# Hybrid diffusion backbone: the state chain's products as one block matrix or as two 64x64 tiles

## The chip, the cores and the metric

The kernel runs on one core of one Trainium2 chip. The metric is the device time of one execution in microseconds, lower is better. A time is the median of several runs; beside it stands one execution that was taken with the hardware profiler, from which all rows below come.

## The reference

One layer of a diffusion backbone over 256 context and 1024 latent tokens, width 1024, in float32. Three token mixers work beside each other on slices of the width (a recurrent mixer with 4 heads of 64, neighbourhood attention with 8 heads, a gated short convolution), one projection joins them, and a product-key expert layer follows. The part that matters here is the recurrent mixer. It keeps, for each head and each of two directions, a 64x64 state `S` that runs over the tokens:

```python
def step(S, inp):
    r_t, kk_t, v_t, w_t, b_t, k_t = inp
    sa = jnp.einsum('bhij,bhj->bhi', S, kk_t)
    S = S * w_t[:, :, None, :] - sa[..., None] * b_t[:, :, None, :] + v_t[..., None] * k_t[:, :, None, :]
    return S, jnp.einsum('bhij,bhj->bhi', S, r_t)
```

The state starts at zero, runs over the context and then over the latent tokens, forward in one direction and backward in the other. The outputs of the latent tokens from both directions are added and normalised.

## The kernel before, in words

The kernel turns the token-by-token recurrence into chunks of 64 tokens. `batch(step, d)` (from line 459 on) treats four chunks of one direction `d`: step 0 is the context, steps 1 to 4 are the latent tokens, so there are ten batches. The two heads of a pair share the 128 partitions: head 0 on partitions 0 to 63, head 1 on 64 to 127, and the index `h` runs over the two pairs. Matrices of a chunk are therefore 128x128 with two 64x64 blocks on the diagonal and zeros elsewhere. They are made by masks (`bn`, `gk`, L555), by transposes of block tiles (`kt`, and the first half of `bn`, L572 and L573), or by additions into the diagonal blocks of a tile that was cleared once (`pr`, L638 to L645).

A batch first builds its operands (lines 467 to 578), solves a triangular system (L580 to L630: `lp`, `lt`, `lx`, `x12`) and makes the transfer matrix `pr`. Only then comes the state chain, lines 649 to 669, which is what the change touches. For each of the four chunks and each pair `h` it makes the new state `M` from three products that gather in one region of PSUM (`mc`, from `kt`, `bn` and `pr`; L658, L659, L661), which ScalarE scales into SBUF (L663). For latent batches it also makes the chunk's output from three products (`yc`, from `gk`, `bn` and `pr`; L667 to L669). The third product of each trio reads the state that the chunk before left. The operand held in the array is the 128x128 block matrix; the moved operand has 64 columns. All of them are float32. Work of other kinds stands beside the batches in the program: the input projections (`pj`, L158 to L160), the neighbourhood attention (`pw`, `pc`, `pt`, `po`, L806 to L839) and, after the last batch, the rest of the projections, the output projection and the expert layer with its gathers.

The order of instructions on each engine is not written by hand. The tile framework plans it by simulating the program, so products of several batches, of the projections and of the attention stand mixed on TensorE's queue, which TensorE works off in order (its weight loads run ahead of its products). Waits between engines are semaphores that the framework places; in a trio only the last product signals ScalarE.

Of the kernel before, what the change touches and what calls it, by code (L numbers as in the profile page):

```python
# [19 lines left out]
P = 128  # L20
# [34 lines left out]
def hybrid_kernel(ctx: ExitStack, tc: tile.TileContext, A: dict, out: bass.AP, dbg=None):  # L55
    nc = tc.nc
# [118 lines left out]
    def bank(name, tag):  # L175
        return pw1.tile([P, 512], F32, tag=tag, name=name, bufs=NBANK[tag])
# [67 lines left out]
    for m in range(8, 16, 2):  # L244
        w = sm_.tile([P, 2, KD, P], F32, tag="aw", name=f"aw{m}", bufs=4)
        nc.sync.dma_start(w, A["ada_w"][:, m - 8:m - 6])
        ps = bank(f"ada{m}", "ra")
        for j in range(2):
            for k in range(KD):
                nc.tensor.matmul(ps[:, 2 * j:2 * j + 2], w[:, j, k, :], scc[:, k, :],  # L250
                                 start=k == 0, stop=k == KD - 1)
# [187 lines left out]
    def rot(name, shape, n, init=lambda t: nc.vector.memset(t, 0.0)):  # L439

        if name not in RN:
            ts = [cw.tile(shape, F32, name=f"{name}{i}") for i in range(n)]
            for t in ts:
                init(t)
            RN[name] = [ts, 0]
        r = RN[name]
        r[1] += 1
        return r[0][(r[1] - 1) % n]
# [7 lines left out]
    def b2(ap):  # L456
        return ap.unsqueeze(2).to_broadcast([P, 4, 2, 64])

    def batch(step, d):
        g = 0 if step == 0 else (step if d == 0 else 5 - step)  # L460
        c0, t0, lat = 4 * g, 256 * g, g > 0
# [12 lines left out]
        for h in range(2):  # L474
            ci = 2 * d + h

            def gt(name, shape, bufs=1, h=h):
                return gp.tile(shape, F32, tag=name, name=f"{name}_{step}{d}{h}", bufs=bufs)
# [12 lines left out]
            if last:  # L491
                rb = rot("kx", [P, 4, P], 1)
                bps = bank(f"bo{g}{h}", "ra")
                for a in range(2):
                    q_ = slice(64 * a, 64 * a + 64)
# [56 lines left out]
            bn, gk = gt("bn", [P, 4, 256], 4), gt("gk", [P, 4, P], 4)  # L552
# [14 lines left out]
            kt = gt("kt", [P, 4, P], 4)  # L567
            rx = gt("rx", [P, 4, 192], 3)
            for src, dst in ((kx, rx[:, :, 0:P]), (bb, bn[:, :, 0:P]), (kb, kt)):
                ps = bank(f"tr_{step}{ci}", "ra")  # L570
# [3 lines left out]
            ps = bank(f"lkv_{step}{ci}", "ra")  # L574
# [13 lines left out]
        for h in range(2):  # L588
            s, ci = S[h], 2 * d + h
# [5 lines left out]
            ps = bank(f"x0_{step}{ci}", "rb")  # L595
# [6 lines left out]
        for l in range(2):  # L602
            for h in range(2):
                s, ci = S[h], 2 * d + h
                ps = bank(f"lp_{step}{ci}{l}", "rb")
                for u in range(4):
                    nc.tensor.matmul(ps[:, u * P:(u + 1) * P], s["E"][:, u, :], s["X"][:, u, :], start=True, stop=True)
                pm = s["gt"]("pm", [P, 4, P])
                nc.vector.tensor_mul(pm, ps.rearrange("p (c b) -> p c b", c=4),
                                     cst[:, C_L16 + l, :].unsqueeze(1).to_broadcast([P, 4, P]))  # L610
                ps = bank(f"lt_{step}{ci}{l}", "rb")
# [8 lines left out]
        for h in range(2):  # L620
            s, ci = S[h], 2 * d + h
            x12 = s["gt"]("x12", [P, 4, 192], 2)
            for u2 in range(2):
                ps = bank(f"x12_{step}{ci}{u2}", "rb")
                for j in range(2):
                    u = 2 * u2 + j
# [3 lines left out]
        for h in range(2):  # L630
            s, ci = S[h], 2 * d + h
            pr = rot("pr", [P, 4, 256], 2)
            na_ = 2 if lat else 1
            for u2 in range(2):
                ps = bank(f"pr_{step}{ci}{u2}", "rb")
                for j in range(2):
                    u = 2 * u2 + j
                    nc.tensor.matmul(ps[:, j * 256:j * 256 + na_ * P], s["x12"][:, u, 0:P], s["bn"][:, u, :na_ * P], start=True, stop=True)  # L638
                us = slice(2 * u2, 2 * u2 + 2)
                for a in range(2):  # L640
                    q_ = slice(64 * a, 64 * a + 64)
# [8 lines left out]
        for i in range(4):  # L650
            for h in range(2):
                s, ci = S[h], 2 * d + h
                u = i if d == 0 else 3 - i
                v_, x2_ = s["vS"][:, u, :], s["x12"][:, u, P:]
                M = Mst.get(ci)
                if step < 4 or i < 3:
                    pm = mch[:, h * 256 + u * 64:h * 256 + u * 64 + 64]
                    nc.tensor.matmul(pm, s["kt"][:, u, :], v_, start=True, stop=False)  # L658
                    nc.tensor.matmul(pm, s["bn"][:, u, 0:P], x2_, start=False, stop=M is None)  # L659
                    if M is not None:  # L660
                        nc.tensor.matmul(pm, s["pr"][:, u, 0:P], M, start=False, stop=True)  # L661
                    Mn = gp.tile([P, 64], F32, tag=f"M{ci}", name=f"M_{step}{ci}{i}", bufs=2)
                    nc.scalar.activation(Mn, pm, AF.Copy, scale=s["tot"][:, u:u + 1])  # L663
                    Mst[ci] = Mn
                if lat:
                    py = ych[:, h * 256 + u * 64:h * 256 + u * 64 + 64]
                    nc.tensor.matmul(py, s["gk"][:, u, :], v_, start=True, stop=False)  # L667
                    nc.tensor.matmul(py, s["bn"][:, u, P:], x2_, start=False, stop=False)
                    nc.tensor.matmul(py, s["pr"][:, u, P:], M, start=False, stop=True)  # L669
        if not lat:  # L670
            return
        if last:
# [29 lines left out]
        for h in range(2):  # L702
            yd = rot("yd", [P, 4, P], 1)
            for a in range(2):
                q_ = slice(64 * a, 64 * a + 64)
                nc.vector.tensor_add(yd[q_, :, q_], vb[h][q_], y[q_, h])
            ps = bank(f"yo{h}{g}", "ch")
# [3 lines left out]
        nc.sync.dma_start(d_y[:, 0:2, tl:tl + 256], gs)  # L711

    batch(0, 0)
    batch(0, 1)
    rwkv_inputs(TBLK[1])
    batch(1, 0)
    load_h(*TBLK[2], 0)
    rwkv_inputs(TBLK[2])
# [369 lines left out]
    for q in range(2):  # L1088
        ps = bank(f"g2{q}", "pj")
# [191 lines left out]
    for e in range(P):  # L1281
# [16 lines left out]
        for t0, n in DBLK:  # L1298
            ps = bank(f"ds{e}_{t0}", "pj" if opened or t0 else "rb")[:, :n]
# [40 lines left out]
    for g in range(NGRP):  # L1340
# [20 lines left out]
        if g == NGRP - 1:  # L1361
            fins, fgen, ends = (), None, list(ENDS)
            for x, i in enumerate(LAST):
                if i < len(stay):
                    acc_of(i, stay[i], False, True)
                else:
                    ps = bank(f"dq{g}{i}", "ch")
# [13 lines left out]
        for r in range(nr):  # L1381
            ps = bank(f"dq{g}{r}", "ch")
# [100 lines left out]
```

## Time and profile before

| what | value |
|---|---|
| median of 3 runs | 3696.5 us (3678.78 to 3700.78) |
| profiled execution | 3709.2 us, span 3707.4 us |
| TensorE busy (products) | 3357.4 us, 91% |
| VectorE busy | 2921.6 us, 79% |
| ScalarE busy | 1564.8 us, 42% |
| GpSimd busy | 1391.3 us, 38% |
| mean granted TensorE clock | 0.95 |

In the rows, PE is TensorE's products and PEld its weight loads, DVE is VectorE, ACT ScalarE, POOL GpSimd. A row names the line, the operation, what it writes and what it reads (buffer numbers left out). A count such as x8 is the number of instructions. The duration of a product contains its way through the array, so products overlap each other in the rows; their pace is read from the starts of successive rows. The granted clock is a share of full speed: 1.00 is 2.4 GHz, 0.50 is 1.2 GHz.

### The profile page before, as it was taken

Reading aid. Unit: us, or ns where it says so; the run is one execution under the profiler, and the core shown is the slowest. Engines: PE = TensorE matmul, PEld = TensorE weight load, DVE = VectorE, ACT = ScalarE, POOL = GpSimd, SP = SyncE. Lnnn points to the kernel's source line nnn. Section 1 sums busy time; section 2 is a strip of 40 time slices with the busy share of each in tenths; the row PEclk is TensorE's granted clock in tenths of the full one; section 3 lists DMA queues with packets and bytes.
Section 4 is the critical chain, followed back from the end, with each engine's and each line's share of the span. In section 5 each row is a group of like instructions: output and inputs, shape, how many; then the busy total and the mean of one; then the engine's idle time right before and its main releaser. Section 6 shows DMA issues by size and latency. Waiting matters only on the chain.

```text
span 3707.4 us, 55747 instructions
## 1 busy us (share of the span) xinstructions
PE 3357.4 (91%) x19927; PEld 3031.5 (82%) x19927; DVE 2921.6 (79%) x6275; ACT 1564.8 (42%) x3039; POOL 1391.3 (38%) x1100
## 2 busy tenths in 40 slices
PE   7698898897879878989899999999998999999997
PEld 6587787886868757989899999999986778888885
DVE  7566657785685648989879999999876888888888
ACT  3453333442434433246244676676632333233332
POOL 3343232110053223445433335455542544443343
PEclk9899998998989889989999999999998999999998
DMA  6435543221565645798887879999998999999996
GB/s 249 129 114 163 161 138 96 65 64 55 171 198 170 205 163 174 272 312 304 299 281 260 284 287 347 344 367 369 341 353 300 345 339 340 345 346 349 339 345 230
DMA packets 405784, 928.08 MB, mean 250 GB/s; under 512 B 45569, under 2 KB 182145, under 8 KB 399873
## 3 DMA queue, kind: packets, MB, share of 16 engines
q1 hardware_dynamic: 248064, 408.81, 34.1%
q0 software_dynamic: 111920, 407.95, 30.6%
q10 hardware_dynamic: 45520, 107.76, 7.5%
q8 instruction: 157, 2.57, 0.3%
q14 instruction: 123, 1.00, 0.1%
HBM read 802.74 MB, written 121.63 MB: 249 GB/s over the span
## 4 chain that ended last, share of the span: by engine, by line
PE 31%; DVE 14%; DMA 8%; issue 7%; POOL 1%; ACT 1%; SPq 1%; DVEq 0%; ACTq 0%; POOLq 0%
PE ds L160 4%; PE ds L158 4%; PE ds L159 4%; DVE ru L1152 4%; PE dp L158 4%; PE dp L159 4%; PE dp L160 4%; PE gm L1067 2%; PE dq L159 2%; PE dq L160 2%; PE dq L158 2%; DMA rv<-in_peer_v_dram,idx 1%; DMA dws<-d_ge 1%; DMA ru<-in_peer_u_dram,idx 1%; DVE acc L1163 1%
## 5 line engine op out<-in xcount | busy, mean ns | idle before, releaser
L1135 POOL DMA_INDIRECT ru<-in_peer_u_dram,idx x384 | 513.8, 1338 | 735.2 <-ACT dqs L1387 172.7
L1135 POOL DMA_INDIRECT rv<-in_peer_v_dram,idx x384 | 498.8, 1299 | 700.5 <-ACT dqs L1387 237.0
L1152 DVE CUSTOM_DVE_ANT_0 ru<-ru,h 128x1024 f32<-128x1024 f32 x384 | 471.7, 1242 | 87.3 <-DMA ru<-in_peer_u_dram,idx 84.5
L1163 DVE SCALAR_TENSOR_TENSOR acc<-rv,gw,acc 128x1024 f32<-128x1024 f32 x381 | 488.7, 1283 | 38.0 <-DMA rv<-in_peer_v_dram,idx 34.4
L159 PE MATMUL dp<-dvls,dwhs 128*128 128x512 f32 x896 | 349.7, 391 | 1.1 <-DVE dvls L1269 1.1
L160 PE MATMUL dp<-dvhs,dwls 128*128 128x512 f32 x896 | 347.2, 390 | 0.0
L158 PE MATMUL dp<-dvhs,dwhs 128*128 128x512 f32 x896 | 318.7, 395 | 0.0
L208 POOL TENSOR_TENSOR wl<-w,wh 128x1024 fp32r<-128x1024 f32 x68 | 166.4, 2451 | 300.8 <-ACT wh L206 291.2
L158 PE MATMUL pj<-hbh,wh 128*128 128x512 f32 (+1 forms) x544 | 216.5, 399 | 19.5 <-ACT wh L206 13.8
L1302 ACT ACTIVATE ge<-ds 128x256 f32<-128x256 f32 (+1 forms) x256 | 111.1, 434 | 268.6 <-PE ds L160 221.8
L160 PE MATMUL pj<-hbh,wl 128*128 128x512 f32 (+1 forms) x544 | 213.8, 394 | 2.0 <-POOL wl L208 1.9
L159 PE MATMUL pj<-hbl,wh 128*128 128x512 f32 (+1 forms) x544 | 212.5, 391 | 2.1 <-POOL hbl L189 2.1
L158 PEld LDWEIGHTS dp<-dvhs,dwhs 128*128 128x128 f32 x896 | 171.1, 191 | 35.6
L159 PEld LDWEIGHTS dp<-dvls,dwhs 128*128 128x128 f32 x896 | 169.5, 189 | 36.9 <-DVE dvls L1269 1.5
L1272 ACT CAST dwhs<-dws 128x640 fp32r<-128x640 f32 x128 | 91.4, 731 | 254.0 <-DVE dws L1271 124.2
L160 PEld LDWEIGHTS dp<-dvhs,dwls 128*128 128x128 f32 x896 | 169.1, 189 | 35.3
L158 PE MATMUL dq<-dvhs,dwhs 128*128 128x512 f32 x384 | 151.3, 394 | 25.6 <-ACT dvhs L1268 23.6
L1269 DVE TENSOR_TENSOR dvls<-dvs,dvhs 128x1024 fp32r<-128x1024 f32 x128 | 155.3, 1220 | 24.5 <-ACT dvhs L1268 24.2
L1268 ACT CAST dvhs<-dvs 128x1024 fp32r<-128x1024 f32 x128 | 133.0, 1052 | 83.2 <-DMA dvs<-in_peer_v_dram 79.1
L1067 PE MATMUL gm<-oa,ob 128*128 128x128 f32 x1280 | 156.9, 275 | 1.6 <-DVE oa L1054 1.1
L1387 ACT COPY dqs<-dq 128x512 f32<-128x512 f32 x90 | 52.8, 587 | 249.7 <-PE dq L160 242.9
L1067 PEld LDWEIGHTS gm<-oa,ob 128*128 128x128 f32 x1280 | 152.5, 192 | 2.5 <-issue 1.4
(1990 smaller groups left out, 10266.1 us busy)
## 6 DMA issues: line engine op xcount, KB each, us to landing
du<-in_peer_ut_dram SPq DMA_DIRECT2D x128, 512.0 KB
dvs<-in_peer_v_dram SPq DMA_DIRECT2D x128, 512.0 KB
d_ge<-ge ACTq DMA_DIRECT2D x128, 320.0 KB
d_g<-gt ACTq DMA_DIRECT2D x40, 1024.0 KB
dgs<-d_g SPq DMA_DIRECT2D x32, 1280.0 KB
dws<-d_ge SPq DMA_DIRECT2D x128, 320.0 KB
w<-in_w_in_dram SPq DMA_DIRECT2D x68, 512.0 KB
wq<-in_q_w_dram SPq DMA_DIRECT2D x48, 512.0 KB
```

Source lines behind the costliest of these rows:

```text
L158: nc.tensor.matmul(ps, lh_, rh_, start=start, stop=False)
L159: nc.tensor.matmul(ps, lh_, rl_, start=False, stop=False)
L160: nc.tensor.matmul(ps, ll_, rh_, start=False, stop=stop)
L208: WE[0].tensor_tensor(wl, w, wh.bitcast(F32), op=OP.subtract)
L1067: nc.tensor.matmul(ps[:, t * P:(t + 1) * P], ob[:, q + t], oa[:, q + t], start=True, stop=True)
L1135: paced(nc.gpsimd.indirect_dma_start(out=r, out_offset=None, in_=A[tab], in_offset=bass.IndirectOffsetOnAxis(ap=idx[:, tt, s:s + 1], axis=0)))
L1152: yield from rows("peer_u", tt, lambda s, u: nc.vector.tensor_tensor_reduce(u, u, h2, 1.0, 0.0, OP.mult, OP.add, act[:, s:s + 1]))
L1163: nc.vector.scalar_tensor_tensor(acc, v, w[:, s:s + 1], acc, op0=OP.mult, op1=OP.add)
L1268: nc.scalar.copy(vh, v)
L1269: sv = nc.vector.tensor_tensor(vl, v, vh.bitcast(F32), op=OP.subtract)
L1272: nc.scalar.copy(wh, wt)
L1302: ev = nc.scalar.activation(ge[:, t0:t0 + n], ps, AF.Gelu_apprx_tanh)
```

## The change

Each product of the chain is issued twice, once for each head: the 64x64 block of the held operand against the 64 partitions of the moved operand, into the 64 partitions of the result. The order of the three terms stays, and within a term head 0 comes before head 1. Nothing else changes.

```diff
+    def heads2(ps, terms):
+
+        for i, (lt, rt) in enumerate(terms):
+            for a in range(2):
+                q_ = slice(64 * a, 64 * a + 64)
+                nc.tensor.matmul(ps[q_], lt[q_, q_], rt[q_], start=i == 0, stop=i == len(terms) - 1)
...
                 if step < 4 or i < 3:
                     pm = mch[:, h * 256 + u * 64:h * 256 + u * 64 + 64]
-                    nc.tensor.matmul(pm, s["kt"][:, u, :], v_, start=True, stop=False)
-                    nc.tensor.matmul(pm, s["bn"][:, u, 0:P], x2_, start=False, stop=M is None)
-                    if M is not None:
-                        nc.tensor.matmul(pm, s["pr"][:, u, 0:P], M, start=False, stop=True)
+                    heads2(pm, ((s["kt"][:, u, :], v_), (s["bn"][:, u, 0:P], x2_)) + (() if M is None else ((s["pr"][:, u, 0:P], M),)))
                     Mn = gp.tile([P, 64], F32, tag=f"M{ci}", name=f"M_{step}{ci}{i}", bufs=2)
                     nc.scalar.activation(Mn, pm, AF.Copy, scale=s["tot"][:, u:u + 1])
                     Mst[ci] = Mn
                 if lat:
                     py = ych[:, h * 256 + u * 64:h * 256 + u * 64 + 64]
-                    nc.tensor.matmul(py, s["gk"][:, u, :], v_, start=True, stop=False)
-                    nc.tensor.matmul(py, s["bn"][:, u, P:], x2_, start=False, stop=False)
-                    nc.tensor.matmul(py, s["pr"][:, u, P:], M, start=False, stop=True)
+                    heads2(py, ((s["gk"][:, u, :], v_), (s["bn"][:, u, P:], x2_), (s["pr"][:, u, P:], M)))
```

## Rows read from the trace of the kernel before

**Rows 1.** The page's first part: busy us, share of the span, instructions.
```profile
PE 3357.4 (91%) x19927; PEld 3031.5 (82%) x19927; DVE 2921.6 (79%) x6275; ACT 1564.8 (42%) x3039; POOL 1391.3 (38%) x1100
```
**Rows 2.** Busy time by stretch: us, each engine (instructions), PEclk, DMA share, GB/s.
```profile
250.00:905.00 655.00, 575.01 (x3847) 524.74 (x3845) 430.60 (x1208) 242.16 (x551) 151.76 (x175) 0.94 0.35 104
905.00:1385.00 480.00, 388.19 (x2252) 339.08 (x2253) 306.81 (x887) 199.79 (x388) 135.75 (x89) 0.87 0.58 179
756.00:760.00 4.00, 4.00 (x21) 4.00 (x21) 2.41 (x9) 0.81 (x2) 2.69 (x5) 0.51 0.49 146
```
**Rows 3.** TensorE's longest wait, 250 to 905 us: total, times, longest.
```profile
PE lt L613 <- DVE pm L609: 19.9, 7, 7.1
```
**Rows 4.** The chain's instructions by line: duration ns min/median/max, first and last start.
```profile
L658 PE MATMUL mc<-vS,kt x152: 217/273/421, 256.7 to 898.6; 128*128 128x64 f32 x152
L659 PE MATMUL mc<-x,bn x152: 275/275/421, 256.9 to 898.8; 128*128 128x64 f32 x152
L661 PE MATMUL mc<-M,pr x144: 275/275/421, 265.5 to 899.1; 128*128 128x64 f32 x144
L663 ACT ACTIVATE M<-mc,tots x76: 301/315/344, 258.1 to 899.4; 128x64 f32<-128x64 f32 x76
...
L667 PE MATMUL yc<-vS,gk x128: 219/275/421, 289.8 to 899.5; 128*128 128x64 f32 x128
L668 PE MATMUL yc<-x,bn x128: 219/275/287, 424.3 to 899.7; 128*128 128x64 f32 x128
L669 PE MATMUL yc<-M,pr x128: 219/275/422, 436.5 to 900.0; 128*128 128x64 f32 x128
```
**Rows 5.** Timeline of the last chain, one period: start us, us, engine, line, operation.
```profile
891.80 0.39 PE L658 MATMUL mc<-vS,kt 128*128 128x64 f32 x2
...
892.25 0.39 PE L661 MATMUL mc<-M,pr 128*128 128x64 f32 x2
...
892.67 0.31 ACT L663 ACTIVATE M<-mc,tots 128x64 f32<-128x64 f32 x1 [4.92 <-PE mc L661]
...
893.14 0.39 PE L658 MATMUL mc<-vS,kt 128*128 128x64 f32 x2
```
**Rows 6.** Timeline of TensorE's products, at 710 us and at 757 us.
```profile
710.12 1.00 PE L498 MATMUL bo<-cst,kx 128*128 128x2 f32 x8
710.98 0.85 PE L826 MATMUL pt<-cst,s 128*128 128x128 f32 x6
711.67 1.06 PE L613 MATMUL lt<-XT,pm 128*128 128x128 f32 x8
712.57 0.82 PE L627 MATMUL x<-rx,XT 128*128 128x192 f32 x4
...
756.80 1.92 PE L613 MATMUL lt<-XT,pm 128*128 128x128 f32 x8
758.51 1.72 PE L617 MATMUL lx<-pm,XT 128*128 128x128 f32 x8
```
**Rows 7.** Timeline of TensorE's products, where the chain meets other work, 744 us.
```profile
744.21 0.36 PE L806 MATMUL pw<-kh,qs 128*128 128x256 f32 x1
744.41 0.33 PE L658 MATMUL mc<-vS,kt 128*128 128x64 f32 x2
744.58 0.39 PE L659 MATMUL mc<-x,bn 128*128 128x64 f32 x2
...
745.02 0.39 PE L669 MATMUL yc<-M,pr 128*128 128x64 f32 x2
745.22 0.36 PE L807 MATMUL pw<-kl,qs 128*128 128x256 f32 x1
...
746.12 0.44 PE L658 MATMUL mc<-vS,kt 128*128 128x64 f32 x2
746.39 0.39 PE L659 MATMUL mc<-x,bn 128*128 128x64 f32 x2
```
**Rows 8.** Timeline of TensorE's weight loads, the start after a wait.
```profile
746.12 0.30 PEld L658 LDWEIGHTS mc<-vS,kt 128*128 128x128 f32 x2 [0.27 <-ACT M L663]
```

## The prediction

> **What bounds the kernel now.** I read the page's first part, then the busy time by stretch, then the waits of TensorE, then the rows of the edited lines. TensorE is the busiest engine over the whole span, with 91% [rows 1]. The products that the change touches all lie in the stage of the recurrent mixer, 250 to 905 us. There TensorE is busy for 575.0 of 655 us, 88%, and no other engine passes 66% [rows 2]. So its queue, which it works off in order, sets the stage: other batches, projections and attention stand between the products of the chain and fill the time in which those wait. The 80 us that are left are mostly waits inside the solve of a batch; the largest is 19.9 us, for the masked product on VectorE [rows 3]. The chain's own products hardly show there. ScalarE's step that makes the next state waits for TensorE, not the other way round. What TensorE gains or loses in these products therefore goes into the stage's end at nearly full size. I take 0.88 of it, the busy share, since the other 12% is slack in which a shorter or longer piece may vanish. The profile can't show that the delay reaches the end of the kernel, but the output of this stage is an input of everything after it, and TensorE is 81% busy in the next stretch too [rows 2], so I pass it on whole.
>
> **What the products cost.** Each call in float32 appears as two pairs of a weight load and a matmul, since lines 658 to 669 show 152, 152, 144 and three times 128 pairs, and only 76 new states [rows 4]. That is 832 pairs from 416 calls. In the last chain, where nothing else is on the chip, one chunk's six products for both head pairs (12 pairs) take 893.14 - 891.80 = 1.34 us [rows 5], 0.112 us a pair. All of them: 832 x 0.112 = 93 us of TensorE.
>
> What sets 0.112? Pairs that move 2 columns take (710.98 - 710.12) / 8 = 0.108 us, pairs that move 128 take (712.57 - 711.67) / 8 = 0.112, and pairs of 64, above, the same [rows 6]. So it isn't the moved columns. At the lower clock (0.51 in 756 to 760 us [rows 2]) the pair takes (758.51 - 756.80) / 8 = 0.214 us [rows 6], almost twice as much, so it isn't a cost of issuing either, which would not follow that clock. What these pairs share is the load of a 128-column operand.
>
> **The change, part by part.** It removes 416 calls and adds 832, each with half the rows, half the columns loaded, and the same 64 columns moved: 1,664 pairs in place of 832. ScalarE's step, the semaphore that releases it, the planes of PSUM and all DMAs stay. The result of a product is the same, since the block matrices hold zeros outside the two heads' blocks. No wait is added: the last pair of a group is still the one that releases ScalarE.
>
> *Price of a pair.* No row shows a load of fewer than 128 columns, so I bound it. Upper end: the load doesn't get shorter, and 1,664 x 0.112 = 186 us, +93. Lower end: a load of 64 columns takes half, 0.056 us, and the loads of the two tiles go side by side: 832 x 0.056 = 47 us, -47. Between them: half as long, and one after the other, as all loads here come: 1,664 x 0.056 = 93 us, no change. I take this one, since it is nearest to what rows show (work in proportion to the clock, one load behind the other). A fixed part beside it follows from the two clocks: twice 0.112 less 0.214 is 0.010 us by the pairs of 128 columns, and about nothing by those of 2. For the 832 extra pairs that is 0 to 8 us; I take +4.
>
> *Going in and out of the tiles.* The 832 pairs stand in 90 unbroken runs on TensorE's queue, between the first of 256.7 us and the last, of 80 pairs, at 891.2 us; 37 of them are of 12 pairs. So there would be some 180 changes between the whole array and its tiles. Lower end: nothing. A run begins 0.20 us after a product of another form and width, and the next begins 0.20 us after its last two pairs, without a gap (744.21 to 744.41, 745.02 to 745.22) [rows 7]. Upper end: TensorE must empty itself first. A product's latency is 275 ns at the median [rows 4], 0.163 us beyond its share of 0.112. And a load that couldn't be taken ahead shows its price once: after a wait for the state the first two pairs took 746.39 - 746.12 = 0.27 us [rows 7, 8], against 744.58 - 744.41 = 0.17 us otherwise: 0.10 us. Together 0.26 us a change, 47 us in all. I take one such uncovered load per run, 90 x 0.10 = 9 us, between the ends but nearer to the rows without a gap.
>
> The Trainium skill, in TensorEngine Tiling (Array Packing), Key Properties, says that a change of the tiling mode, as against a change of tile, drains TensorE. No run here shows it; by it the upper end of this term would hold, and it is the second rival below. The same section says that tiles are independent and can run weight loads and matmuls in parallel; by that the lower end of the pair's price would hold, the first rival below. The trace has no second tile to agree or disagree with.
>
> *Cover.* The latency of the chain itself costs nothing so far: ScalarE's step takes 0.31 us in a period of 1.34 [rows 5], beside products that don't need the new state. That cover stays, since the products of the state against the rest come last in the group as before. Were it gone, each step would wait 0.31 us for ScalarE and some more, 76 steps, at most 24 us, of which most lie beside other work.
>
> *Order.* The order of the queues comes from a planner that simulates the program. With other instructions it may place batches and projections differently. The whole idle time of the stage is 80 us [rows 2]; I give a reordering 15 us either way.
>
> **The sum.** (4 + 9) x 0.88 = +11 us. The profiled execution took 3709.2 us around a span of 3707.4, so it would take 3720. It stands 12.7 us above the median of the runs, 3696.5; on the median the forecast is 3707.5. A measurement of this kernel tells about 1%, 37 us, from no change, so this is no change.
>
> **The rivals.**
> 1. *The tiles load side by side.* The queue would hold 47 us less; with 9 for the changes, (9 - 47) x 0.88 = -33, 3663. For it: the two tiles share neither rows nor columns of the array. Against it: no row shows two loads at a time. With the dear changes of rival 2 as well, it ends near zero, which I count with the forecast.
> 2. *Every change of mode empties the array* (the other side). Place: the 90 runs between products of the whole array. Price: 47 us of uncovered latency and load, plus 4, times 0.88 = +45, 3741. For it: the runs are short, mostly 12 pairs or fewer. Against it: today's changes of form and width leave no gap [rows 7]. It decides from about 0.2 us a change; below that the result stays within 1%.
> 3. *A load costs the same for 64 columns.* +93 and 9, times 0.88 = +90, 3786. For it: pairs of all widths cost the same [rows 6]. Against it: that row varies only the moved columns.
> 4. The clock falls. It is 0.94 on the mean in this stage [rows 2], so it falls now and then already. No row says what products on tiles do to it; half of the chain's 93 us at the lower clock would add 47 us. It goes into the upper part of the range with rival 2.
>
> **How the numbers follow.** Forecast (loads in turn, changes cheap, or both effects dear and cancelling): 0.48, within about 15 us of 3707. Rival 1: 0.22, of which half falls below the 1% mark of 3660. Rivals 2 and 4: 0.20, most of it above 3733. Rival 3: 0.10. Range 3655 to 3745: it takes in the forecast, most of rival 1 and half of what lies above rival 2's price, and leaves out rival 3 and the tails. The chances: faster 0.12, the half of rival 1 with a little of reordering; slower 0.26, rival 3, most of rivals 2 and 4; the rest, 0.62, is within 1%.
>
> **What would show it.** Right: in the last, undisturbed chain a chunk for both head pairs still takes about 1.34 us with 24 pairs of 64 columns, 0.056 us apart, and the stage's end moves by less than 20 us. Rival 1: that period falls towards 0.7 to 0.9 us, until ScalarE's step shows as TensorE's wait. Rival 2: idle time of TensorE just before the first pair of each run and before the first whole-array load after it. Rival 3: a period of about 2.7 us. Rival 4: a granted clock well under 0.94 in the stage. The sum is wrong if TensorE's products shorten and the stage's end doesn't move, for then the waits in the solve were the bound.

## The result and the profile after

The changed kernel takes 3669.3 us (median of 5 runs, 3663.1 to 3677.9) where the kernel before, in 5 runs beside it, takes 3696.5: a ratio of 0.9937, 95% interval 0.9913 to 0.9960, so 23 us or 0.6% less. That is within the 1% that the prediction called no change and inside its range, but on the other side of zero from its sum of +11 us.

The page's first part of the kernel after:

```profile
span 3667.5 us, 57401 instructions
PE 3334.0 (91%) x20759; PEld 2986.6 (81%) x20759; DVE 2905.2 (79%) x6275; ACT 1561.9 (43%) x3038; POOL 1398.4 (38%) x1100
```

TensorE has 832 more products and loads than in [rows 1], and less busy time. The span is 39.9 us shorter than that of before, but the profiled execution of before stood 12.7 us above its median and this one is its median, so 27 us is what the two have to explain.

The chain's instructions, listed by tile (duration ns min/median/max, first and last start):

```profile
L464 PEld LDWEIGHTS mc<-vS,kt x304: 129/132/228, 252.0 to 878.7; 64*64 64x64 f32 x152
L464 PE MATMUL mc<-vS,kt x304: 218/218/366, 252.0 to 878.7; 64*64 64x64 f32 x152
...
L667 ACT ACTIVATE M<-mc,tots x76: 296/315/350, 253.4 to 879.3; 128x64 f32<-128x64 f32 x76
...
L464 PE MATMUL yc<-M,pr x256: 218/218/311, 425.1 to 879.8; 64*64 64x64 f32 x128
```

Against [rows 4] there are twice as many products, as the change says; each is 218 ns long instead of 275. The chain ends at 879.8 us, 20.2 us earlier than the 900.0 of before. (It also began 4.7 us earlier, ahead of anything that was edited.) Behind the chain 18.7 us were left at the last projection (1211.3 against 1230.0) and 27.1 at the first expert product (1483.4 against 1510.5).

How fast the pairs go stands in the timeline of the last chain, one period (start us, us, engine, line, operation, and in brackets the idle time and what ended it):

```profile
876.60 0.19 PEld L464 LDWEIGHTS mc<-vS,kt 64*64 64x64 f32 x4 [0.20 <-ACT M L667]
876.60 0.33 PE L464 MATMUL mc<-vS,kt 64*64 64x64 f32 x4
...
876.77 0.28 PE L464 MATMUL mc<-x,bn 64*64 64x64 f32 x4
...
876.88 0.28 PE L464 MATMUL mc<-M,pr 64*64 64x64 f32 x4
...
877.00 0.28 PE L464 MATMUL yc<-M,pr 64*64 64x64 f32 x4
...
877.12 0.28 PE L464 MATMUL yc<-vS,gk 64*64 64x64 f32 x4
...
877.21 0.32 ACT L667 ACTIVATE M<-mc,tots 128x64 f32<-128x64 f32 x1 [0.67 <-PE mc L464]
877.23 0.28 PE L464 MATMUL yc<-x,bn 64*64 64x64 f32 x4
...
877.58 0.33 PE L464 MATMUL mc<-vS,kt 64*64 64x64 f32 x4
```

Four pairs (two heads, two passes) start every 0.11 to 0.12 us: 877.23 - 876.77 = 0.46 us for sixteen, 0.029 us a pair. A product for both heads costs half of what it did. The period fell from the 1.34 us of [rows 5] to 877.58 - 876.60 = 0.98, of which the 24 pairs take about 0.70; then TensorE stands and waits for the new state. ScalarE's step, which was hidden, now shows as 0.20 us of idle time in each period of this undisturbed chain. In the busy stage it hardly does: the waits of TensorE for `M` are 1.6 us there, against 1.1 before.

What going in and out of the tiles costs stands in a busier place, in the same view, TensorE's products:

```profile
523.71 0.38 PE L614 MATMUL lp<-X,E 128*128 128x128 f32 x2
524.02 0.33 PE L464 MATMUL mc<-vS,kt 64*64 64x64 f32 x4
524.18 0.28 PE L464 MATMUL mc<-x,bn 64*64 64x64 f32 x4
524.30 0.28 PE L464 MATMUL mc<-M,pr 64*64 64x64 f32 x4
...
524.65 0.28 PE L464 MATMUL yc<-x,bn 64*64 64x64 f32 x4
524.86 0.71 PE L614 MATMUL lp<-X,E 128*128 128x128 f32 x4
```

and its weight loads:

```profile
523.59 0.31 PEld L614 LDWEIGHTS lp<-X,E 128*128 128x128 f32 x2
524.02 0.19 PEld L464 LDWEIGHTS mc<-vS,kt 64*64 64x64 f32 x4
524.13 0.20 PEld L464 LDWEIGHTS mc<-x,bn 64*64 64x64 f32 x4
...
524.86 0.63 PEld L614 LDWEIGHTS lp<-X,E 128*128 128x128 f32 x5
```

Within a run the loads are ahead of the products (524.13 against 524.18). At both ends they aren't: the first tile load and the first tile product begin together, and so do the first whole load and product behind the run. The second `lp` product starts at 523.81; without a change of mode the first tile product could follow 0.11 us later. From there to 524.86 are 0.94 us for 24 pairs that need 0.70. So one run costs 0.24 us for going in and out together. The 1,664 pairs stand in 97 unbroken runs. Counted in the same way, the 76 of them that have no wait and the full granted clock cost 0.24 us at the median; and at all 97 the first product, on the way in as on the way out, starts within 0.03 us of its load.

Both prices give the queue: 1,664 x 0.029 + 97 x 0.24 = 48 + 23 = 71.5 us where 93 stood, 21.5 less, and at the prediction's 0.88 a gain of 19 us. The busy time by stretch from the first chain product to the last, in the kernel before and in the kernel after:

```profile
256.70:900.00 643.30, 568.07 (x3807) 518.84 (x3805) 422.21 (x1185) 238.56 (x546) 151.76 (x175) 0.94 0.35 105
252.00:879.80 627.80, 562.44 (x4639) 491.26 (x4638) 418.61 (x1185) 238.11 (x546) 152.64 (x175) 0.93 0.36 108
```

The stage is 15.5 us shorter at a clock lower by 0.01. Length times granted clock is my estimate of the stage at full speed, good to some 3 us because the clock is given to two places; it falls from 605 to 584, by 21. That the chain's end came 20.2 us earlier, nearly the 19, is in part luck, since 4.7 of it lie ahead of the chain.

By stretch, as in [rows 2]:

```profile
250.00:905.00 655.00, 574.78 (x4682) 500.34 (x4680) 433.02 (x1226) 241.89 (x553) 152.64 (x175) 0.91 0.36 108
```

The same 655 us now hold the stage and 25 us of what follows, and the granted clock is 0.91 over them.

### The profile page after: what moved, and what is told of

Read it like the earlier page. It is cut to its first block, busy times and chain, and to the rows that moved or that the text cites. A ratio compares the mean times of both kernels' runs of the same rounds, so it can differ in the third digit from the quotient of the medians.

```text
span 3667.5 us, 57401 instructions
## 1 busy us (share of the span) xinstructions
PE 3334.0 (91%) x20759; PEld 2986.6 (81%) x20759; DVE 2905.2 (79%) x6275; ACT 1561.9 (43%) x3038; POOL 1398.4 (38%) x1100
## 4 chain that ended last, share of the span: by engine, by line
PE 37%; DVE 14%; DMA 5%; issue 4%; ACT 1%; POOL 1%; SPq 1%; ACTq 0%; DVEq 0%; POOLq 0%
PE dp L158 5%; PE dp L159 5%; PE dp L160 5%; PE ds L160 4%; PE ds L158 4%; PE ds L159 4%; DVE ru L1154 4%; PE gm L1069 2%; PE dq L158 2%; PE dq L159 2%; PE dq L160 2%; DVE acc L1165 1%; DMA rv<-in_peer_v_dram,idx 1%; DVE oa L1056 1%; DMA dws<-d_ge 1%
## 5 line engine op out<-in xcount | busy, mean ns | idle before, releaser
L1137 POOL DMA_INDIRECT ru<-in_peer_u_dram,idx x384 | 504.4, 1314 | 728.1 <-ACT dqs L1389 166.8
L1137 POOL DMA_INDIRECT rv<-in_peer_v_dram,idx x384 | 510.6, 1330 | 682.2 <-ACT dqs L1389 247.0
L1154 DVE CUSTOM_DVE_ANT_0 ru<-ru,h 128x1024 f32<-128x1024 f32 x384 | 475.7, 1254 | 82.1 <-DMA ru<-in_peer_u_dram,idx 81.9
```

Source lines behind the costliest of these rows:

```text
L1137: paced(nc.gpsimd.indirect_dma_start(out=r, out_offset=None, in_=A[tab], in_offset=bass.IndirectOffsetOnAxis(ap=idx[:, tt, s:s + 1], axis=0)))
L1154: yield from rows("peer_u", tt, lambda s, u: nc.vector.tensor_tensor_reduce(u, u, h2, 1.0, 0.0, OP.mult, OP.add, act[:, s:s + 1]))
```

## The experiments

The theory: the two tiles work side by side, 0.029 us a pair, because they share neither rows nor columns of the array; a run of them costs 0.24 us to enter and leave; and what the queue gains or loses reaches the end nearly whole. Its rivals: that the gain comes from another order of the planner rather than from the tiles, that the changes of mode cost nothing, or that the queue isn't the bound. In the expectations A is the theory and B the rival that the run is to tell from it, as each text says. Edits are against the kernel after, unless another is named. A time is set against the kernel before on the same chip, with the ratio and its 95% interval.

**Head by head, not term by term.**

```diff
-        for i, (lt, rt) in enumerate(terms):
-            for a in range(2):
+        for a in range(2):
+            for i, (lt, rt) in enumerate(terms):
```

> The same tile products, but all terms of head 0 of a trio first, then all of head 1, so that neighbours on the queue mostly share a tile. Theory A (only neighbouring products of different tiles run side by side): a trio of 12 pairs takes about 12 x 0.056 = 0.67 us, as the whole-array form does, with a little overlap where the tiles change; the gain of the changed kernel is lost and the in-and-out cost of the runs stays, so 10 to 20 us slower than before. Rival B (the engine looks far enough ahead to run both tiles' queues side by side whatever the order): a trio still takes about 0.35 us and the time stays with the changed kernel's, 0.6% below before.

3681.6 us, 0.9964 (0.9948 to 0.9980). The timeline of TensorE's products, last chain:

```profile
875.55 0.33 PE L464 MATMUL mc<-vS,kt 64*64 64x64 f32 x2
...
876.12 0.28 PE L464 MATMUL yc<-vS,gk 64*64 64x64 f32 x2
876.24 0.22 PE L464 MATMUL yc<-x,bn 64*64 64x64 f32 x1
876.25 0.27 PE L464 MATMUL yc<-vS,gk 64*64 64x64 f32 x1
876.30 0.22 PE L464 MATMUL yc<-x,bn 64*64 64x64 f32 x1
...
876.69 0.32 PE L464 MATMUL mc<-vS,kt 64*64 64x64 f32 x2
```

A period of 1.14 us; the 24 pairs themselves take 0.915 us, 0.038 each. Three products of one tile in a row let the other tile wait, yet not all the way to the 0.056 us of loads in turn: it lies between the two expectations. The two heads next to each other, as in the change, are worth something. The rows also settle a rival that the theory leaves open, that a 64x64 load takes a quarter of a 128x128 one (it holds a quarter as many numbers) and the loads still go in turn: while one tile has the queue to itself, its pairs start 0.06 us apart (two from 876.12 to 876.24), and when the other tile's first pair comes, it starts 0.01 us behind (876.25). So a pair of one tile takes about 0.058 us, half of a whole one, and 0.029 is two tiles at once.

**Two column halves, the same rows.** Both tiles take all 128 rows; the zeros of the block matrix are multiplied again.

```diff
-                nc.tensor.matmul(ps[q_], lt[q_, q_], rt[q_], start=i == 0, stop=i == len(terms) - 1)
+                nc.tensor.matmul(ps[q_], lt[:, q_], rt, start=i == 0, stop=i == len(terms) - 1)
```

> Each head's product takes all 128 rows (the held block beside the zeros of the other head) and 64 columns, so the two tiles share the rows and differ in columns only; the result is the same. Theory A (loads go side by side because the tiles share no rows): now they share rows, loads go in turn, a call costs 4 x 0.056 = 0.22 us as before, and the in-and-out cost of the runs is left over: 10 to 25 us slower than before. Rival B (different columns suffice): a call costs about 0.12 us and the time is the changed kernel's, about 0.6% below before.

3679.7 us, 0.9953 (0.9938 to 0.9969). Timeline, last chain:

```profile
870.64 0.34 PE L464 MATMUL mc<-vS,kt 128*64 128x64 f32 x4
870.81 0.29 PE L464 MATMUL mc<-x,bn 128*64 128x64 f32 x4
870.92 0.29 PE L464 MATMUL mc<-M,pr 128*64 128x64 f32 x4
...
871.63 0.34 PE L464 MATMUL mc<-vS,kt 128*64 128x64 f32 x4
```

The run of 24 pairs takes 0.697 us, as with 64x64 tiles, and the period is 0.99; in time it is level with the change, within the intervals. So the reason that I gave was too narrow: the two tiles needn't differ in rows. Different columns suffice. Whether different rows alone would do was not tried, since both heads would then gather in the same partitions.

**Only the state, only the outputs.** One of the two trios stays whole (`whole` is one matmul per term with the full operands).

```diff
-                    heads2(py, ((s["gk"][:, u, :], v_), (s["bn"][:, u, P:], x2_), (s["pr"][:, u, P:], M)))
+                    whole(py, ((s["gk"][:, u, :], v_), (s["bn"][:, u, P:], x2_), (s["pr"][:, u, P:], M)))
```

> Only the state's trios (448 of the 832 pairs of before) are made on tiles, the outputs' trios stay whole. Theory A (a call halves, and each run on tiles costs about 0.26 us going in and out): the queue saves 448 x 0.056 = 25 us and pays 0.26 us for each of about 76 runs, 20 us, since a state's trio now stands between whole products: within 10 us of before. Rival B (going in and out is nearly free and the saving was smaller for another reason): about 20 us faster than before.

3690.5 us, 0.9986 (0.9970 to 1.0003); 76 runs of tiles. The other way round, with `pm` whole and `py` on tiles:

> Only the outputs' trios (384 of the 832 pairs of before) are made on tiles, the state's trios stay whole. Theory A: the queue saves 384 x 0.056 = 21 us and pays 0.26 us for each of about 64 to 75 runs, 17 to 20 us: within 10 us of before. Rival B (going in and out is nearly free): about 18 us faster than before.

3699.8 us, 1.0005 (0.9989 to 1.0020); 92 runs. In the total, half of the products on tiles brings far less than half of the gain: there are half the pairs, but nearly as many changes of mode. Both totals came out as the theory had it, and the price of a run, read from their traces as above, is 0.24 us in both (63 and 79 runs). Their stages alone fell by more, as the table further down shows.

**The middle term whole.** Each trio now goes tile, whole, tile.

```diff
+            if i == 1:
+                nc.tensor.matmul(ps, lt, rt, start=False, stop=i == len(terms) - 1)
+                continue
```

> The middle product of every trio (the one with bn) goes back to the whole array, the first and third stay on tiles, so each of the 140 trios gets one more way out of the tiles and in again. Theory A (a run on tiles costs 0.2 to 0.3 us going in and out, and a call on tiles half a whole one): 140 x 0.25 = 35 us more in the queue, and 140 calls at 0.11 us more, 15 us; 50 us in all, so 40 us or more above the changed kernel, 10 to 25 us slower than before. Rival B (going in and out is nearly free): only the 15 us, still about 12 us faster than before.

3709.1 us, 1.0035 (1.0019 to 1.0052): 13 us slower than the kernel with no tiles at all, though two thirds of the pairs are cheaper. Runs of tiles rose from 97 to 172, not by the one per trio that the source suggests, since the planner put neighbouring trios together. Against the kernel after it is 36 us longer, where 40 or more were expected for 140 more runs; 75 more came. A change of mode costs time on the path to the end.

**The output trio twice.** The second trio overwrites the first, so the result stays.

```diff
+                    for _ in range(2):
+                        heads2(py, ((s["gk"][:, u, :], v_), (s["bn"][:, u, P:], x2_), (s["pr"][:, u, P:], M)))
```

> The changed kernel with every output trio made twice, the second time over the first (same result): 64 x 12 = 768 more pairs on tiles, no further run. It asks how much of TensorE's queue in this stage reaches the end. Theory A (the queue bounds the stage at about 0.88, and a pair on tiles takes 0.029 us): 768 x 0.029 = 22 us, so 15 to 22 us above the changed kernel, 5 to 12 us faster than before. Rival B (waits of the solve bound the stage, the queue has room): within 6 us of the changed kernel, about 25 us faster than before.

3698.3 us, 1.0013 (0.9991 to 1.0034). The 768 added pairs and 8 more runs are 24 us on the queue; against the kernel after (0.9937) the time is 0.76%, 28 us, longer, and the two intervals leave some 12 us either way. That is more than the 15 to 22 expected, and the kernel is no faster than before. The rival's 6 us are clearly out. The stage, from the first chain product to the last:

```profile
256.40:898.30 641.90, 574.88 (x5405) 501.78 (x5406) 420.34 (x1185) 237.87 (x546) 152.44 (x175) 0.95 0.35 106
```

At full speed that is 610 us, against 584 in the kernel after, 26 more. So what is added to TensorE's queue in this stage comes out at its end at about full size; 0.88 and 1 can't be told apart by this.

**The order alone, and the change again in that order.** In the kernel before, the first two terms of each trio change places:

```diff
-                    nc.tensor.matmul(pm, s["kt"][:, u, :], v_, start=True, stop=False)
-                    nc.tensor.matmul(pm, s["bn"][:, u, 0:P], x2_, start=False, stop=M is None)
+                    nc.tensor.matmul(pm, s["bn"][:, u, 0:P], x2_, start=True, stop=False)
+                    nc.tensor.matmul(pm, s["kt"][:, u, :], v_, start=False, stop=M is None)
```

> The kernel before, with the first two terms of every trio in the other order and all on the whole array: nothing is added or saved, but the planner gets another program. It asks how much another order alone is worth. Theory A (order is worth little): within 6 us of before. Rival B (the planner's order explains differences of 10 us and more, and so part of what the changed kernel gained): more than 8 us from before, either way.

3683.8 us, 0.9975 (0.9957 to 0.9993): the same work, 9 us less, by the planner's order alone. That is on the rival's side, though the interval (3 to 16 us) reaches into the theory's 6. The kernel after with the same exchange:

> The changed kernel with the first two terms of every trio in the other order: against the run with the same order on the whole array (terms swapped, 0.25% faster than before) it is the change once more under another plan of the queues. Theory A (the tiles themselves save about 20 us of TensorE's queue, the order is worth about 10 either way): 15 to 30 us below that run, so 0.7 to 1.0% faster than before. Rival B (the changed kernel's gain was mostly a lucky order): within 8 us of that run.

3691.7 us, 0.9978 (0.9962 to 0.9995). In this pair the tiles gain nothing in the total (1 us more, some 9 either way), as the rival had it and against the theory. Where they gain, and where that went, the busy time by stretch tells, from the first chain product to the last, of the kernel before with exchanged terms:

```profile
248.00:874.90 626.90, 564.36 (x3806) 514.16 (x3805) 417.54 (x1185) 238.22 (x546) 153.74 (x175) 0.95 0.36 108
```

and of the kernel after with exchanged terms:

```profile
256.70:878.50 621.80, 556.19 (x4639) 484.57 (x4638) 413.51 (x1185) 238.04 (x546) 152.99 (x175) 0.93 0.36 109
```

The stage is 5 us shorter at a clock lower by 0.02; length times granted clock falls from 596 to 578. The total lost it again elsewhere: the chain began 8.7 us later, and from the first expert product to the first product of its next part (`ds` to `dq`) this execution took 1262 us, that of its counterpart 1254, and over all kernels here that untouched stretch took between 1233 and 1262.

**Outputs ahead of the state.** In the kernel before, the output trio is moved ahead of the trio for the new state, so that ScalarE's step comes last; then the same in the kernel after:

```diff
+                if lat:
+                    py = ych[:, h * 256 + u * 64:h * 256 + u * 64 + 64]
+                    heads2(py, ((s["gk"][:, u, :], v_), (s["bn"][:, u, P:], x2_), (s["pr"][:, u, P:], M)))
                 if step < 4 or i < 3:
...
-                if lat:
-                    py = ych[:, h * 256 + u * 64:h * 256 + u * 64 + 64]
-                    heads2(py, ((s["gk"][:, u, :], v_), (s["bn"][:, u, P:], x2_), (s["pr"][:, u, P:], M)))
```

> The kernel before, all on the whole array, with each chunk's output trio issued ahead of its state trio; no work is added or saved. A second sample of what another order alone is worth: Theory A: within 12 us of before, either way. Rival B (order is worth more than the change): further off than 15 us.

3691.4 us, 0.9985 (0.9968 to 1.0003), without tiles. With them:

> The changed kernel with each chunk's output trio issued ahead of its state trio: the change a third time, against the run with the outputs first on the whole array. Theory A (the tiles save about 20 us): 15 to 30 us below that run. Rival B (order): within 8 us of it.

3667.4 us (6 runs, 3661.5 to 3677.1), 0.9917 (0.9897 to 0.9937), the fastest of these kernels, ahead of the kernel before by 0.8%. Its lead over the changed kernel is within the intervals. The tiles are worth 0.68%, 25 us, in this order. The stage of the first,

```profile
256.80:900.00 643.20, 572.33 (x3807) 522.19 (x3805) 418.15 (x1185) 238.67 (x546) 151.82 (x175) 0.93 0.34 105
```

and of the second:

```profile
245.50:869.70 624.20, 561.89 (x4639) 490.54 (x4638) 417.25 (x1185) 237.97 (x546) 152.72 (x175) 0.93 0.35 108
```

19 us, at one clock. So in the three orders the stage, at full speed, lost 21, 17 and 18 us, while the totals lost 23, nothing and 25. The order alone moves the same estimate by 9 and 7 us (596 and 598 in the two kernels without tiles, against 605 before), so each of these is uncertain by about as much.

**All products of the batches head by head.** Not the chain alone: the operands, the solve and the transfer matrix too are kept as packed 64x64 blocks (masks, `E`, `X`, `XT`, `x12`, `bn`, `kt`, `gk`, `pr`), and their products all go through `heads2`. One edit for many:

```diff
-                    nc.tensor.matmul(ps[:, u * P:(u + 1) * P], s["E"][:, u, :], s["X"][:, u, :], start=True, stop=True)
-                pm = s["gt"]("pm", [P, 4, P])
+                    heads2(ps[:, u * 64:(u + 1) * 64], ((s["E"][:, u, :], s["X"][:, u, :]),))
+                pm = s["gt"]("pmc", [P, 4, 64])
```

> All products of the mixer's batches by head on tiles (operands, transposes as products with the identity, solve, transfer matrices, chain, output), with operands and results kept as packed 64x64 blocks, so that the solve's products move 64 columns instead of 128, x12 128 instead of 192 and pr 128 instead of 256, and the masks and copies on VectorE, ScalarE and GpSimd handle half the elements; the projections and the attention stay whole. Theory A (a call with 64 columns on two tiles takes half of a whole one): lp, lt and lx save 720 pairs x 0.056 = 40 us, pr and x12 about 20, lkv, bo and yo about 15, the chain 47, against some 0.25 us for each of 100 to 200 runs; with the shorter waits for VectorE 60 to 110 us faster than before. Rival B (the runs get so many and short that going in and out eats it): within 20 us of the changed kernel.

3710.8 us, 1.0036 (1.0017 to 1.0054), slower, with 6,400 pairs on tiles. Neither expectation held: it is no faster than before, and some 37 us slower than the changed kernel, further from it than the rival's 20. The chain ends at 762.4 us, 138 earlier than before; but the input projections that follow begin behind 925 us in both kernels, and the last of them starts no earlier (1229.1 against 1230.0), so all of it is gone there. The stretches up to the chain's end, from there to 925, and from 0 to 925:

```profile
225.40:762.40 537.00, 456.66 (x6671) 384.36 (x6668) 315.83 (x962) 177.39 (x395) 125.69 (x143) 0.93 0.38 112
762.40:925.00 162.60, 108.52 (x466) 87.92 (x465) 61.86 (x196) 50.24 (x126) 14.48 (x8) 0.53 0.34 100
0.00:925.00 925.00, 728.93 (x8350) 602.15 (x8351) 527.28 (x1485) 326.48 (x692) 223.03 (x222) 0.83 0.40 126
```

The attention, which filled the chain's gaps before, was left over and ran by itself, with waits, and the granted clock was 0.53. Two rows of TensorE's timeline from there:

```profile
804.02 1.81 PE L811 MATMUL pt<-cst,s 128*128 128x128 f32 x6 [1.82 <-ACT s L801]
806.75 2.83 PE L817 MATMUL po<-vN,pT 128*128 128x64 f32 x12 [0.92 <-ACT pT L813]
```

The same twelve `po` products take 1.45 us at 743 us in the kernel before.

**The same, with the attention pulled into the stage** by the planner's priorities; the products stay.

```diff
-    load_h(*TBLK[1], 1)
+    with tc.high_priority(offset=5000):
+        load_h(*TBLK[1], 1)
...
-        drain(attend(na, range(0, 2), 0, 512, ("pj", "pj", "pj", "pj"), (2, 2, 1, 2, 1)))
+        with tc.high_priority(offset=2000):
+            drain(attend(na, range(0, 2), 0, 512, ("pj", "pj", "pj", "pj"), (2, 2, 1, 2, 1)))
```

> The kernel with all products of the mixer on tiles, whose chain ended 138 us earlier than before's (762 against 900 us) but left the attention of the first tokens to run alone behind it at the lower clock, and the same projections ending at the same time as before; here the planner gets the order to take the later projections 5000 and that attention 2000 places earlier, so that they stand between the mixer's products again. No work differs. Theory A (the saved time was lost because the work that fills TensorE's gaps came too late and then ran alone): 50 to 110 us faster than before. Rival B (something else ends this part of the kernel, a transfer or another engine): within 15 us of the run without the order, so no faster than before.

3694.0 us, 0.9989 (0.9977 to 1.0000): 17 us better than without the priorities, and yet level with the kernel before, where 50 to 110 us less were expected. From the start to the first output projection:

```profile
0.00:908.20 908.20, 722.33 (x8326) 600.46 (x8326) 510.77 (x1485) 320.91 (x688) 223.03 (x222) 0.86 0.40 126
```

against, in the kernel before,

```profile
0.00:924.80 924.80, 778.96 (x4807) 690.61 (x4807) 610.44 (x1570) 357.79 (x748) 250.69 (x262) 0.92 0.39 123
```

TensorE's busy time is 57 us less, the end only 17 earlier, and the granted clock fell from 0.92 to 0.86. By length times clock the stretch went from 851 to 781 us at full speed; in plain time, TensorE stood idle for 186 us instead of 146. So the saved work was there, and a lower clock and longer waits took most of it back. How much each took isn't shown, nor that the clock fell because TensorE had less to do: no run set the one against the other, and the rival, that something else ends this part, stays open.

## Why the prediction was wrong

What bounds the kernel was read rightly. TensorE's queue sets the stage, and gains and losses there reach the end: 24 us added moved the time by 28, and the stage at full speed by 26. Whether 0.88 or 1 is the better share, these numbers can't tell. The measured time lies inside the range, but not by the case that the forecast was built on.

The step that failed is the *price of a pair*. Of the three values, loads at full price, half as long in turn, and half as long side by side, I took the middle one, 0.056 us a tile pair, as "nearest to what rows show". Measured: 0.029. That is rival 1, at which I put 0.22. Its point for it, that the tiles share neither rows nor columns, was good evidence on the very question; against it I had only that no row shows two loads at once, and none could, since the kernel had no second tile. A missing row was taken for a row against. Half of that point would have done, since different columns suffice. So about -45 stood where I put +4, for the fixed part isn't seen either.

*Going in and out* was under-sized by the same reasoning on the other side. I took 0.10 us a run, one uncovered load; measured is 0.24 a run, on 97 runs 23 us instead of 9. The rows without a gap [rows 7] showed changes of form between whole products and said nothing on a change of mode. The 0.10 itself was misread: it set the 0.27 us of two pairs after a wait against a pair of 0.17, but two pairs in a row take 0.22 (four from 891.80 to 892.25 [rows 5]), so an uncovered load cost 0.05. Rival 2 had half of the mechanism (loads aren't taken ahead over the change) and over-sized it: 0.26 us a change, where it is about 0.12. The Trainium skill, in TensorEngine Tiling (Array Packing), Key Properties, says that different tiles can run weight loads and matmuls in parallel; the trace agrees (0.029 us a pair with two tiles, 0.058 with one). It also says that a change of mode drains TensorE. Here each change has its price, but that the array is empty at it is not shown: by the rows the last whole product ends at 523.71 + 0.38 = 524.09, behind the start of the first tile product at 524.02 (ends are modelled).

Both rivals at once give -45 + 23, times 0.88, -19. The prediction named that case ("with the dear changes of rival 2 as well, it ends near zero") and counted it with the forecast. With the sizes that came out it isn't near zero.

*Cover* held in the busy stage and went in the last chain, where the period ended in ScalarE's step at 0.98 us, a little above the 0.7 to 0.9 that "what would show it" had for rival 1. *Order* held without tiles: 9 and 6 us by an exchange of terms or of trios alone, inside the 15 that I gave. With tiles it is worth more: the changed kernel in its three orders stands at 0.9937, 0.9978 and 0.9917, up to 23 us apart. The *clock* (rival 4) went from 0.94 to 0.93 in the stage, some 6 us of its length.

The two prices, taken from the kernel after, can be tried on the other runs. Worked out is (pairs on tiles x 0.029 + whole pairs x 0.112 + runs x 0.24 - 93) x 0.88 (for head by head 0.038 a pair, as measured there); beside it stand the difference in total, from the ratio to the kernel before, and the difference of the stage at full speed (its length x clock behind it), all in us:

| kernel | tile pairs, whole pairs, runs | worked out | total | stage at full speed |
|---|---|---|---|---|
| after | 1664, 0, 97 | -19 | -23 | -21 (627.8 x 0.93) |
| head by head | 1664, 0, 97 | -6 | -13 | -10 (625.8 x 0.95) |
| column halves | 1664, 0, 97 | -19 | -17 | -18 (617.8 x 0.95) |
| state only | 896, 384, 76 | -5 | -5 | -16 (619.2 x 0.95) |
| outputs only | 768, 448, 92 | +1 | +2 | -6 (629.9 x 0.95) |
| middle term whole | 1104, 280, 172 | +10 | +13 | +2 (638.7 x 0.95) |
| output trio twice | 2432, 0, 105 | +2 | +5 | +5 (641.9 x 0.95) |
| outputs first (against its own order without tiles) | 1664, 0, 97 | -19 | -25 | -18 (624.2 x 0.93) |
| terms exchanged (against its own order without tiles) | 1664, 0, 91 | -20 | +1 | -17 (621.8 x 0.93) |

In total all but the last agree to 7 us, which is about what an interval leaves open. The last shows what the total of a planned program can hide: its stage shortened like the others, and what lies ahead of it and behind it grew. By the stage the rows with all of the chain on tiles agree to 4 us, but the three that mix tiles and whole products come out 7 to 11 lower than worked out. So the agreement of their totals is partly luck: the expert stretch took 1255 and 1257 us in the first two, 1236 in the kernel before. An order worth 7 to 9 us to the stage could explain it; that isn't shown. Why the expert stretch differs by up to 29 us between kernels with the same instructions in it stays open.

## What to carry to other kernels

In this kernel's float32 products a block-diagonal one made as two 64-column tiles costs half if the two tiles alternate on the queue, and each stretch of such products pays a fixed 0.24 us to enter and leave, which a run earns back from about five whole pairs on (0.112 - 2 x 0.029 = 0.054 us saved on each): so count the unbroken runs on the queue before the pairs, and keep whole-array work out of them. Where a cost has no row because the kernel lacks the thing, the middle between two bounds is no estimate; combine the bounds as cases, and give the corner cases their own chances. And a gain of half a per cent in one stage is read from that stage, with its clock, since the order that a planner finds moves the total by as much (23 us between two orders of the changed kernel).

## What the runs showed of the hardware

- Tiles with the same 128 rows and different 64 columns keep the full pace of two separate tiles: 24 pairs in 0.697 us, as with 64x64.
- Pairs of one 64x64 tile alone start 0.058 us apart, half of a whole pair's 0.112; two tiles that alternate run at once, 0.029 a pair. Three products of one tile ahead of three of the other overlap in part: 0.038.
- Loads aren't taken ahead over a change between the whole array and its tiles, in either direction, at any of the 97 runs; inside a run they are. In and out together cost 0.24 us.
- Where work was taken from TensorE's queue and the place wasn't filled, the granted clock was lower (0.86 against 0.92 up to the output projections, 0.53 where the attention ran alone), and of 57 us less busy time 17 were seen. That the one caused the other isn't shown.
